# Attention values as seven block products in a decoder block kernel, with the second pair's gates and scores behind them

## The chip, the cores and the metric

The kernel runs on one core of one Trainium2 chip. The metric is the device time of one execution in microseconds. TensorE (PE) does the matmuls and transposes, VectorE (DVE) and ScalarE (ACT) the elementwise work, GpSimd (POOL) a few small steps, and SyncE (SP) issues nearly all transfers.

## What is computed

One decoder layer on x (512 x 1024, float32). One wide projection gives nine parts; two token mixers work on them, and their gated sum goes through two matmul stages with layer norms:

```
p = x @ W_in + b_in            # u | v | q | k | value | r | low rank | gate A | gate B
y_A = gelu(u) * (tril(W_s) @ layer_norm(gelu(v)) + b_s)      # in chunks of 128 positions, 8 groups
y_B = rms_norm(gla(q, k, value, log_sigmoid(...) / 16)) * gn * silu(r)    # 4 heads, chunked
m = sigmoid(gate_A) * y_A + sigmoid(gate_B) * y_B
h = layer_norm(alpha * x + m @ W_out)
out = layer_norm(alpha * h + relu(h @ W_1)^2 @ W_2)
```

## The kernel before

Every large matmul is done in three passes of reduced-precision operands: an operand is split into a high part, cast on ScalarE (`split`, line 88), and a low part, a subtraction on VectorE (line 89), and high x high, high x low and low x high are summed in a bank of PSUM. Weights come as a stream of 128 x 1024 pieces (`_stream`, `load_to`, `split_to`): SP loads a raw piece into one of three buffers, and the split fills one of seven pairs `wh`, `wl`. `split_to(n)` makes the pieces up to n, so each unit of matmuls asks for pieces up to seven ahead of its own. In the feed-forward, the second matrix is multiplied in seven block products instead of eight (Strassen-Winograd: `product_of`, `accumulators`, `operand`), with sums of weight pieces (line 128) in four held buffers A0, A1, B0, B1; each product is 24 matmuls.

The first part is a row of jobs, numbered by slots (`slot`), one for each bank of PSUM that is filled: the first q and k (a prologue), v (slots 0 to 7), u (8 to 15), the second pair's q and k (16 to 19), the attention values (20 to 27, two `row_unit`s of 96 matmuls, written to `bufB` by `copy_take`, line 786), gate A (`ga`, 28 to 35), then r and gate B (`r`, `gb`, 36 to 51, two and two: `branch`). A `col_job` is 24 matmuls on one weight piece. Side work is planned into slots by `at(n, f, phase)`: MM after the job's matmuls on TensorE, MAIN behind it, and LATE behind the next weight split. Instructions of TensorE, VectorE, ScalarE and GpSimd stand in the order in which this Python issues them; nothing is reordered there. SP's transfers are placed by a scheduler.

The side work of a pair of heads (`plan_pair`): gates (`gates_a`, `gates_b`), the parts between chunks (`inter_*`, `kd_turn`), three levels of scores (`level_diff`, `level_kdiff`, `level_exp`, `level_prep`, `level_score`: a difference of cumulated gates, its exponential, products with q and k, then eight matmul records `sc`), and diagonal scores (`diag_*`: products `dr`, their cast and low part `dt`, then the matmuls `sd`). Scores are copied into `AT` under masks (lines 501 to 533), and `chunk_out` makes the outputs and states per chunk. The two pairs are `pr0` and `pr1`.

PSUM has eight banks: four main ones (`ps_m`) for the jobs, two for scores and turned values (`ps_s`, one tile at a time), two for other side work (`ps_a`, tag `aux`). `r_take` turns the values' outputs on TensorE (`yt`) into the scores' tile.

## Time and profile before

| | |
|---|---|
| median of 3 runs | 756.06 us (755.71 to 756.31) |
| profiled execution | 755.66 us, span 753.9 us |
| TensorE busy | 745.6 us (99%), 3498 records of matmuls |
| VectorE busy | 473.7 us (63%) |
| ScalarE busy | 343.7 us (46%) |
| DMA | 85.14 MB, 113 GB/s on average |

Busy time is a share of the whole span; stages differ. A matmul of 512 columns is shown with some 0.39 us, but the next starts after 0.227 us, so times on TensorE are read from starts, as the chain does. An operand on a row such as `wl<-raw,wh` is what is written, then what is read.

### The profile page before, as it was taken

To read this page: it belongs to the slowest core of one execution; us is meant where nothing else is said; L and a number is where in the kernel's file an instruction comes from. 1 tells how busy PE (TensorE), PEld (TensorE's weight loads), DVE (VectorE), ACT (ScalarE), POOL (GpSimd) and SP (SyncE) were. 2 spreads that over 40 slices of the span, in tenths; PEclk is the share of its full clock that TensorE was granted. 3 is DMA by queue.
4 is the path that set the end of the run, shared out by engine and by line. 5 is a ranking of instruction groups with operands and counts; after the bars stand their busy time and mean duration, and the time that the engine had idled before them with its cause. 6 is when DMAs were issued, how large, how long until landed. Compare 5 with 4: busy or idle time off the path is not lost.

```text
span 753.9 us, 8782 instructions
## 1 busy us (share of the span) xinstructions
PE 745.6 (99%) x3498; PEld 626.2 (83%) x3498; DVE 473.7 (63%) x592; ACT 343.7 (46%) x450; POOL 29.9 (4%) x60
## 2 busy tenths in 40 slices
PE   9999999999999999999999999999999999999996
PEld 8888888888888888888888988888888888888885
DVE  7379867677575644445468523777567856687645
ACT  7476754363254745454222545454444454445300
POOL 1000000000000112000002000000000000000001
PEclk9999999999999999999999999999999999999998
DMA  8633421222141132522340314145331634145111
GB/s 342 214 124 126 153 82 61 82 84 84 49 146 58 56 126 85 183 96 85 98 159 33 115 62 151 41 140 196 113 111 39 240 107 145 56 121 202 41 57 56
DMA packets 25464, 85.14 MB, mean 113 GB/s; under 512 B 3088, under 2 KB 3344, under 8 KB 25424
## 3 DMA queue, kind: packets, MB, share of 16 engines
q1 hardware_dynamic: 25280, 84.33, 32.9%
q8 instruction: 27, 0.44, 0.2%
q10 hardware_dynamic: 144, 0.26, 0.1%
q14 instruction: 13, 0.11, 0.0%
HBM read 82.48 MB, written 2.10 MB: 112 GB/s over the span
## 4 chain that ended last, share of the span: by engine, by line
PE 97%; issue 1%; DVE 1%; POOL 0%; DVEq 0%; POOLq 0%
PE f L692 22%; PE ps L218 17%; PE mx L975 9%; PE f L1075 6%; PE gb L692 6%; PE r L692 6%; PE ga L692 6%; PE u L692 6%; PE mv L975 4%; PE qk L692 3%; PE first L276 3%; PE m L975 2%; PE sc L520 2%; PE pm L745 1%; PE po L554 1%
## 5 line engine op out<-in xcount | busy, mean ns | idle before, releaser
L89 DVE TENSOR_TENSOR wl<-raw,wh 128x1024 fp32r<-128x1024 f32 x141 | 171.1, 1223 | 114.3 <-ACT wh L88 112.5
L88 ACT CAST wh<-raw 128x1024 fp32r<-128x1024 f32 x141 | 145.6, 1044 | 49.0 <-PE ps L218 23.7
L692 PE MATMUL f<-xh,wh 128*128 128x512 f32 (+1 forms) x288 | 105.4, 366 | 0.0
L692 PE MATMUL f<-xl,wh 128*128 128x512 f32 (+1 forms) x288 | 105.3, 365 | 0.0
L692 PE MATMUL f<-xh,wl 128*128 128x512 f32 (+1 forms) x288 | 105.2, 365 | 0.0
L692 PEld LDWEIGHTS f<-xl,wh 128*128 128x128 f32 x288 | 54.3, 189 | 8.8
L692 PEld LDWEIGHTS f<-xh,wh 128*128 128x128 f32 x288 | 54.3, 189 | 8.7
L692 PEld LDWEIGHTS f<-xh,wl 128*128 128x128 f32 x288 | 54.3, 189 | 8.7
L915 ACT ACTIVATE F<-f 128x512 f32<-128x512 f32 (+1 forms) x28 | 15.0, 537 | 79.9 <-PE f L692 79.1
L218 PE MATMUL ps<-wh,xh 128*128 128x512 f32 x128 | 50.4, 394 | 0.0
L218 PE MATMUL ps<-wh,xl 128*128 128x512 f32 x128 | 49.9, 389 | 0.0
L218 PE MATMUL ps<-wl,xh 128*128 128x512 f32 x128 | 49.8, 389 | 0.0
L975 PE MATMUL mx<-wh,oh 128*128 128x512 f32 x96 | 37.3, 389 | 0.0
L975 PE MATMUL mx<-wl,oh 128*128 128x512 f32 x96 | 37.3, 389 | 0.0
L975 PE MATMUL mx<-wh,ol 128*128 128x512 f32 x96 | 37.3, 389 | 0.0
L128 DVE TENSOR_TENSOR raw<-raw,raw 128x1024 f32<-128x1024 f32 x24 | 29.2, 1218 | 2.8 <-DMA raw<-in_w_all 2.8
L218 PEld LDWEIGHTS ps<-wh,xl 128*128 128x128 f32 x128 | 24.0, 188 | 5.0
L218 PEld LDWEIGHTS ps<-wl,xh 128*128 128x128 f32 x128 | 24.0, 188 | 4.9
L218 PEld LDWEIGHTS ps<-wh,xh 128*128 128x128 f32 x128 | 24.0, 188 | 4.8
L692 PE MATMUL u<-xh,wh 128*128 128x512 f32 x64 | 25.9, 405 | 0.0
L692 PE MATMUL ga<-xh,wh 128*128 128x512 f32 x64 | 25.9, 404 | 0.0
L88 ACT CAST oh<-d 128x1024 fp32r<-128x1024 f32 x12 | 12.6, 1049 | 29.1 <-DVE d L948 29.1
(243 smaller groups left out, 1557.7 us busy)
## 6 DMA issues: line engine op xcount, KB each, us to landing
raw<-in_w_all SPq DMA_DIRECT2D x136, 512.0 KB, 3.3
bufB<-in_head SPq DMA_DIRECT2D x4, 512.0 KB, 7.6
xr<-in_x SPq DMA_DIRECT2D x8, 256.0 KB, 3.6
out<-bufA SPq DMA_DIRECT2D x8, 256.0 KB, 2.0
bufA<-in_head SPq DMA_DIRECT2D x3, 512.0 KB, 5.2
brow<-in_b_in SPq DMA_DIRECT2D x4, 256.0 KB, 6.4
g<-in_ln_g SPq DMA_DIRECT2D x2, 512.0 KB, 5.8
b<-in_ln_b SPq DMA_DIRECT2D x2, 512.0 KB, 5.5
```

The source lines that it names most:

```text
L88: nc.scalar.copy(hi, src)
L89: nc.vector.tensor_tensor(lo, src, hi.bitcast(F32), op=ALU.subtract)
L128: nc.vector.tensor_tensor(raw, x_, y_, op=ALU.subtract)
L218: nc.tensor.matmul(ps, s_, m_, start=(k == 0 and i == 0), stop=(k == KT - 1 and i == 2))
L276: nc.tensor.matmul(first[e], s_, m_[:, k, :], start=(k == 0 and i == 0), stop=(k == KT - 1 and i == 2))
L520: nc.tensor.matmul(sc[:, c, 0:192], pr.kt[:, jc * P : (jc + 1) * P], pr.qt[:, jc, :], start=True, stop=True)
L554: nc.tensor.matmul(po, pr.AT[:, j, c, :], vs, start=True, stop=(c == 0))
L692: nc.tensor.matmul(ps, s_, m_, start=(k == 0 and i == 0), stop=(k == KT - 1 and i == 2))
L745: nc.tensor.matmul(pm[:, c, :], bufB[:, c, gs], wst[:, g, :], start=True, stop=True)
L915: nc.scalar.activation(dst, ps, AF.Relu)
L975: nc.tensor.matmul(ps, s_, m_, start=(begins and k == 0 and i == 0), stop=(k == 3 and i == 2), skip_group_check=True,)
L1075: nc.tensor.matmul(ps, s_, m_, start=(f == 0 and i == 0), stop=(f == 7 and i == 2))
```

## The change

The attention values are computed in the same seven products as the feed-forward's second matrix. Their x operands are quarters of x, transposed, and sums of quarters; raw x is loaded into `bufB` (eight transfers, `operands_begin`) when the mixing has read it, summed there on VectorE (`x_sums`) and split (`x_parts`); weight sums use the held buffers, now open early. Products 1, 6, 7, 4 share main banks x, 5 and 3 main banks v, and product 2 uses the side work's banks (`aux`). Each result is added to a quarter of `bufB` (`value_take`, line 896 there). The look-ahead for weight pieces shrinks from 7 to 4 over the seven products and grows again in the first two `ga` jobs.

The main banks are now four named ones in turn (`bank`), and the turned values `yt` use one of them. The second pair's side work after `gates_a` moves from slots 18 to 35 to slots 25 to 42: behind the values, into `ga` and the first `r` and `gb`. The pair exponential for its diagonal scores is made ahead (`E1`). The order of the gates becomes r0 r1 gb0 gb1 r2 r3 gb2 gb3 gb4 to gb7, then r4 to r7, with the last four gates kept in `bufB`; products with the gate and sums (`onto`) follow.

```diff
-    ps_m = pool(ctx, "ps_m", bufs=4, space=PSUM)
+    ps_m = pool(ctx, "ps_m", bufs=1, space=PSUM)
...
+    turns = [0]
+
+    def bank(name, i=None):
+
+        if i is None:
+            i = turns[0]
+        turns[0] = (i + 1) % 4
+        return ps_m.tile([P, 512], F32, name=name, tag=f"ps{i}")
...
+    vgs = ExitStack()
+    held["pool"] = pool(vgs, "held_v", side="right")
...
+    quarter = lambda a, i, j: a[:, 2 * i : 2 * i + 2, 512 * j : 512 * j + 512]
+    GOES = {1: (0, 0), 2: (0, 0), 5: (1, 1), 6: (0, 1), 3: (0, 1), 7: (1, 1), 4: (1, 0)}
+    NEW = (1, 5, 6, 4)
+    made, sums = {}, {}
+
+    RAW_AT = {(1, 1): (0, 0), (0, 0): (1, 1), (0, 1): (0, 1), (1, 0): (1, 0)}
+
+    def xq(i, j):
+        return quarter(bufB, i, j).rearrange("p a (b n) -> p a b n", n=256)
...
+    def product_of(name, m, ops, take, of, ahead=W_BUFS):
+        hi, lo = ops
+        u0 = unit["next"]
+        unit["next"] = u0 + 2
+        split_to(u0 + 2)
+        banks, begins = accumulators(m, name, of)
...
+            for k in range(4):
...
+                if t and k % 2:
+                    split_to(u0 + k // 2 + 1 + ahead)
+            take(m, t, ps)
...
-        pass
+        E = None
...
+        for j in range(2 if pr.E is not None else 0):
+            nc.scalar.activation(pr.E[:, j, :], par(pr.lf, j, 1), AF.Exp, scale=1.0 / TEMP)
...
-        nc.scalar.activation(pr.raw[:, 512:768], par(pr.lf, j, 1), AF.Exp, scale=1.0 / TEMP)
+        if pr.E is None:
+            nc.scalar.activation(pr.raw[:, 512:768], par(pr.lf, j, 1), AF.Exp, scale=1.0 / TEMP)
...
-        nc.vector.tensor_mul(pair, pair, par(pr.q, j, 1))
+        first_ = pair if pr.E is None else pr.E[:, j, :]
+        nc.vector.tensor_mul(pair, first_, par(pr.q, j, 1))
...
+    def operands_begin():
+
+        sgu.close()
+        vgp = pool(vgs, "vgp", side="left")
+        vgp.tile([P, 120], F32, name="pad_v")
+        for (i, j), (a, b) in RAW_AT.items():
+            for k in range(2):
+                k0 = 4 * j + 2 * k
+                nc.sync.dma_start(xq(a, b)[:, k], head[:, k0 : k0 + 2, 256 * i : 256 * i + 256])
+        return vgp
+
     def second_parts():
-        sgu.close()
+        vgs.close()
+        held.clear()
         pr1.pool = gp1 = pool(gla, "gla_p1", side="left")
         pr1.AT = gp1.tile([P, 2, NCH, P], F32, name="AT1")
         nc.gpsimd.memset(pr1.AT, 0.0)
         pr1.QI = gp1.tile([P, 2, T], F32, name="QI1")
         pr1.KD = gp1.tile([P, 2, NCH, P], F32, name="KD1")
         pr1.et = gp1.tile([P, 2 * NCH], F32, name="et1")
+        pr1.E = gp1.tile([P, 2, T // 2], F32, name="E1")
...
-    S_VG, S_GA = 20, 28
-    S_R, S_O = 36, 52
+    S_VG, S_GA = 20, 27
+    S_R, S_O = 35, 51
...
-    def col_job(name, take):
+    def col_job(name, take, ahead=W_BUFS):
...
-        split_to(u0 + 1 + W_BUFS)
+        split_to(u0 + 1 + ahead)
...
-    at(S_U + 9, second_parts, phase=LATE)
+    at(S_U + 9, lambda: made.update(pool=operands_begin()), phase=LATE)
+    at(S_VG + 6, second_parts)
     at(S_U + 9, lambda: gates_a(pr1), phase=MM)
-    plan_pair(pr1, (18, 19, 20, 21), ((21, 23, 24, 25), (25, 27, 28, 29), (29, 30, 31, 32)), 32)
-    for n, pr, c in [(28, pr0, 0), (31, pr0, 1), (32, pr0, 2), (33, pr0, 3)] + [(36 + c, pr1, c) for c in range(NCH)]:
+    plan_pair(pr1, (25, 26, 27, 28), ((28, 30, 31, 32), (32, 34, 35, 36), (36, 37, 38, 39)), 39)
+    for n, pr, c in [(27, pr0, 0), (30, pr0, 1), (31, pr0, 2), (32, pr0, 3)] + [(43 + c, pr1, c) for c in range(NCH)]:
...
+    X_SUMS = (
+        ((0, 0), (1, 0), (0, 0), ALU.add),
+        ((1, 0), (1, 1), (1, 0), ALU.subtract),
+        ((1, 1), (0, 0), (1, 1), ALU.subtract),
+        ((0, 1), (0, 1), (1, 1), ALU.subtract),
+    )
+
+    def x_sums(n0, n1):
+        for o, a, b, op_ in X_SUMS[n0:n1]:
+            nc.vector.tensor_tensor(quarter(bufB, *o), quarter(bufB, *a), quarter(bufB, *b), op=op_)
+
+    def x_parts(m):
+        hi, lo = (
+            made["pool"].tile([P, 4, 256], F32R, name=f"x{c}{m}", tag=f"x{c}{m in (6, 7)}") for c in "hl"
+        )
+        split(*(a.rearrange("p (a b) n -> p a b n", a=2) for a in (hi, lo)), xq(*{5: (0, 0), 6: (1, 1), 3: (0, 1), 7: (1, 0)}[m]))
+        made[m] = hi, lo
+
+    at(S_VG - 1, lambda: x_sums(0, 1), lambda: x_parts(5))
+    at(S_VG - 1, lambda: x_sums(1, 3), phase=LATE)
...
-    def copy_take(half, br):
-        def f(t, ps):
-            nc.vector.tensor_add(bufB[:, t, half * 512 : (half + 1) * 512], ps, br)
-
-        return f
-
-    for half in range(2):
-        row_unit(xh, xl, copy_take(half, bias_row(C_VG + half * 512)))
+    brs = [bias_row(C_VG + half * 512) for half in range(2)]
+    b0 = turns[0]
+
+    def value_bank(name, kind, t):
+        if kind == "m":
+            return ps_a.tile([P, 512], F32, name=name, tag="aux")
+        return bank(name, (b0 + t + 2 * (kind == "v")) % 4)
+
+    def value_take(m, t, ps):
+        dst = quarter(bufB, *GOES[m])[:, t, :]
+        nc.vector.tensor_add(dst, brs[GOES[m][1]] if m in NEW else dst, ps)
+
+    for n, m in enumerate(ORDER):
+        if m == 5:
+            x_parts(6)
+            x_sums(3, 4)
+        elif m in (6, 3):
+            x_parts({6: 3, 3: 7}[m])
+        if m in (1, 2, 4):
+            i, j = {1: (0, 0), 2: (0, 1), 4: (1, 1)}[m]
+            ops = [a[:, 4 * j : 4 * j + 4, 256 * i : 256 * i + 256] for a in (xh, xl)]
+        else:
+            ops = made.pop(m)
+        product_of(f"v{m}", m, ops, value_take, value_bank, W_BUFS - n // 2)
+        pump(MM, MAIN)
+        pump(LATE)
+    turns[0] = (b0 + 2) % 4
     for e in range(KT):
-        col_job(f"ga{e}", ga_take(e))
+        col_job(f"ga{e}", ga_take(e), W_BUFS - max(0, 2 - e))
...
-            pt = ps_s.tile([P, 2, NCH, P], F32, name=f"yt{e}", tag="sc")[:, 0]
+            pt = bank(f"yt{e}").rearrange("p (c s) -> p c s", s=P)
...
-    def gb_take(e, t1):
+    def onto(e, gate, t1):
+        nc.vector.tensor_mul(t1, t1, gate)
+        nc.vector.tensor_add(AT_[:, e, :], AT_[:, e, :], t1)
+
+    def gb_take(e, gate, t1=None):
         def f(ps):
-            tm = temp(f"gb{e}")
-            nc.scalar.activation(tm, ps, AF.Sigmoid, bias=col("gb", e))
-            nc.vector.tensor_mul(tm, tm, t1)
-            nc.vector.tensor_add(AT_[:, e, :], AT_[:, e, :], tm)
+            nc.scalar.activation(gate, ps, AF.Sigmoid, bias=col("gb", e))
+            if t1 is not None:
+                onto(e, gate, t1)
...
-    def branch(e0):
+    for e0 in (0, 2):
         t1 = {e: temp(f"t1_{e}", "brow") for e in (e0, e0 + 1)}
         for e in t1:
             col_job(f"r{e}", r_take(e, t1[e]))
         for e in t1:
-            col_job(f"gb{e}", gb_take(e, t1[e]))
-            if e0:
-                split(mh[:, e, :], ml[:, e, :], AT_[:, e, :])
-
-    branch(0)
+            col_job(f"gb{e}", gb_take(e, temp(f"gb{e}"), t1[e]))
+
+    gate = {e: bufB[:, e - 4, 0:512] for e in range(4, KT)}
+    for e in gate:
+        col_job(f"gb{e}", gb_take(e, gate[e]))
     gla.close()
...
-    for e in range(2):
+    for e in range(4):
         split(mh[:, e, :], ml[:, e, :], AT_[:, e, :])
-    for e in range(2, KT, 2):
-        branch(e)
+    for e in gate:
+        t1 = temp(f"t1_{e}", "brow")
+        take = r_take(e, t1)
+
+        def parts_take(ps, e=e, t1=t1, take=take):
+            take(ps)
+            onto(e, gate[e], t1)
+            split(mh[:, e, :], ml[:, e, :], AT_[:, e, :])
+
+        col_job(f"r{e}", parts_take)
...
+    def ff_bank(name, kind, t):
+        return bank(name) if kind == "m" else ps_t.tile([P, 512], F32, name=name, tag=f"{kind}{t}")
...
-        b = lambda i, j: f2 + 8 * p + 2 * (2 * (i - 1) + j - 1) + h
+        if p < 0:
+            b = lambda i, j: 20 + 4 * (j - 1) + 2 * (i - 1) + h
+        else:
+            b = lambda i, j: f2 + 8 * p + 2 * (2 * (i - 1) + j - 1) + h
...
+    out += [operand(-1, m, h) for m in ORDER for h in range(2)] + plain(28, n)
...
-    part += [per_tile(w_in[:, c + c0 : c + c0 + 256]) for c0 in range(0, 1024, 256) for c in (C_R, C_GB)]
+    part += [per_tile(w_in[:, c + c0 : c + c0 + 256]) for c0 in (0, 256) for c in (C_R, C_GB)]
+    part += [per_tile(w_in[:, c + 512 : c + 1024]) for c in (C_GB, C_R)]
```

Three places in the order of the instructions. First VectorE at the start of the values. `qt`, `kd` and `QI` belong to the second pair's scores, `wl` are low weight parts, line 786 (896 after the change) takes a result into `bufB`. Before:

```order
L89 TENSOR_TENSOR wl30_1343<-raw30_1208,wh30_1342 128x1024
L786 TENSOR_TENSOR bufB_92<-ps_24_0_1353,brow_1351 128x512
L402 TENSOR_TENSOR QI1_1269<-QI1_1269,q1_1163 128x1024
L403 TENSOR_TENSOR kd1_1340<-kd1_1340,k1_1164 128x1024
L786 TENSOR_TENSOR bufB_92<-ps_24_1_1381,brow_1351 128x512
L425 TENSOR_TENSOR qt1_0_1417<-cum1_1298 128x8x96
L410 COPY KD1_1270<-pt1_0_1407 128x512
L410 COPY KD1_1270<-pt1_1_1412 128x512
L437 TENSOR_TENSOR kt1_0_1421<-cum1_1298 128x1024
```

After the change (`xl5`, `xl6`: low parts of x for products 5 and 6; line 865 sums quarters of x, line 128 weight pieces):

```order
L89 TENSOR_TENSOR xl5_1342<-bufB_92,xh5_1341 128x1024
L128 TENSOR_TENSOR raw25_866<-raw31_1165,raw25_866 128x1024
L89 TENSOR_TENSOR wl30_1346<-raw24_864,wh30_1345 128x1024
L865 TENSOR_TENSOR bufB_92<-bufB_92 128x2x512 x2
L896 TENSOR_TENSOR bufB_92<-brow_1354,mxv1_0_1358 128x512
L89 TENSOR_TENSOR wl31_1380<-raw25_866,wh31_1379 128x1024
L89 TENSOR_TENSOR wl32_1392<-raw30_1163,wh32_1391 128x1024
L896 TENSOR_TENSOR bufB_92<-brow_1354,mxv1_1_1359 128x512
L896 TENSOR_TENSOR bufB_92<-bufB_92,mv2_0_1396 128x512
L128 TENSOR_TENSOR raw30_1163<-raw30_1163,raw34_1312 128x1024
L89 TENSOR_TENSOR wl33_1418<-raw31_1165,wh33_1417 128x1024
L128 TENSOR_TENSOR raw31_1165<-raw31_1165,raw35_1350 128x1024
```

The second pair's products are gone from here, and sums and splits of x and weight sums stand between the takes; two more rows (a weight piece, the second take of product 2) follow before `xl6`.

Second, VectorE between the last level's difference of k (`kt`, line 437, 503 after the change) and its preparation. Before:

```order
L437 TENSOR_TENSOR kt1_2_1772<-cum1_1298 128x1024
L712 TENSOR_TENSOR bufA_91<-bufA_91,ga1_1754 128x512
L458 TENSOR_TENSOR qt1_2_1761<-qt1_2_1761,q1_1163 128x128x6
L460 TENSOR_TENSOR qt1_2_1761<-qt1_2_1761,whole1_2_1774 128x128x4
L460 TENSOR_TENSOR qt1_2_1761<-qt1_2_1761,whole1_2_1774 128x128x2
L465 TENSOR_TENSOR kt1_2_1772<-kt1_2_1772,k1_1164 128x1024
```

After the change:

```order
L503 TENSOR_TENSOR kt1_2_2181<-cum1_1593 128x1024
L935 TENSOR_TENSOR t1_0_2085<-t1_0_2085,gb0_2187 128x512
L936 TENSOR_TENSOR bufA_91<-bufA_91,t1_0_2085 128x512
L524 TENSOR_TENSOR qt1_2_2170<-qt1_2_2170,q1_1170 128x128x6
L526 TENSOR_TENSOR qt1_2_2170<-qt1_2_2170,whole1_2_2183 128x128x4
L526 TENSOR_TENSOR qt1_2_2170<-qt1_2_2170,whole1_2_2183 128x128x2
L531 TENSOR_TENSOR kt1_2_2181<-kt1_2_2181,k1_1171 128x1024
```

Two rows on gate B's first result (`gb0`) stand where one on `ga1` stood.

Third, the second pair's last diagonal score (`dr1_1`, `dt1_1`). ScalarE before:

```order
L711 ACT_TABLE_LOAD
L711 ACTIVATE ga6_2037<-ga6_2012,cols_sb_101 128x512
L482 CAST dt1_1_2044<-dr1_1_2006 128x768
L88 CAST wh45_2048<-raw45_1875 128x1024
L711 ACTIVATE ga7_2083<-ga7_2058,cols_sb_101 128x512
```

ScalarE after the change, and VectorE behind it:

```order
L940 ACT_TABLE_LOAD
L940 ACTIVATE gb2_2364<-gb2_2365,cols_sb_101 128x512
L550 CAST dt1_1_2398<-dr1_1_2362 128x768
L88 CAST wh59_2402<-raw59_2264 128x1024
L940 ACTIVATE gb3_2411<-gb3_2412,cols_sb_101 128x512
```

```order
L935 TENSOR_TENSOR t1_2_2269<-t1_2_2269,gb2_2364 128x512
L936 TENSOR_TENSOR bufA_91<-bufA_91,t1_2_2269 128x512
L548 TENSOR_TENSOR dr1_1_2362<-E1_1645,q1_1170 128x256
L549 TENSOR_TENSOR dr1_1_2362<-dr1_1_2362,k1_1171 128x256
L89 TENSOR_TENSOR wl59_2403<-raw59_2264,wh59_2402 128x1024
L569 COPY_PREDICATED AT1_1640<-masks_283,sd1_0_2393 128x512
L574 COPY_PREDICATED AT1_1640<-masks_283,sd1_0_2393 128x256
L553 TENSOR_TENSOR dt1_1_2398<-dr1_1_2362,dt1_1_2398 128x768
```

The products of `dr1_1` (lines 548 and 549) now stand behind the two rows on `gb2`.

## Rows read from the trace of the kernel before

**Rows 1.** The page, part 4: shares of the chain that ended last, by engine.
```profile
PE 97%; issue 1%; DVE 1%; POOL 0%; DVEq 0%; POOLq 0%
```

**Rows 2.** The chain in order of time (start us, us, what): values, one feed-forward product, last piece.
```profile
159.70 10.88 PE ps L218 x48
...
480.02 5.44 PE m L975 x24
...
703.06 43.84 PE f L1075 x216
```

**Rows 3.** Groups by line and shape: busy us, mean ns of one, idle before.
```profile
L89 DVE TENSOR_TENSOR wl<-raw,wh 128x1024 fp32r<-128x1024 f32 x141 | 171.1, 1223 | 114.3 <-ACT wh L88 112.5
...
L88 ACT CAST wh<-raw 128x1024 fp32r<-128x1024 f32 x141 | 145.6, 1044 | 49.0 <-PE ps L218 23.7 <-DMA raw<-in_w_all 11.3 <-PE mx L975 9.9
...
L786 DVE TENSOR_TENSOR bufB<-ps,brow 128x512 f32<-128x512 f32 x8 | 5.5, 689 | 11.7 <-PE ps L218 11.7
...
L481 DVE TENSOR_TENSOR dr<-dr,k 128x256 f32<-128x256 f32 x4 | 1.7, 426 | 0.1
```

**Rows 4.** Timeline of DVE in the feed-forward (start us, us, engine, line, operation).
```profile
474.35 1.23 DVE L89 TENSOR_TENSOR wl<-raw,wh 128x1024 fp32r<-128x1024 f32 x1
475.49 1.22 DVE L128 TENSOR_TENSOR raw<-raw,raw 128x1024 f32<-128x1024 f32 x1
...
477.76 0.68 DVE L992 SCALAR_TENSOR_TENSOR bufB<-bufA,mx 128x512 f32<-128x512 f32 x1
478.36 1.22 DVE L128 TENSOR_TENSOR raw<-raw,raw 128x1024 f32<-128x1024 f32 x1
```

**Rows 5.** Timelines of DVE, then ACT, around the start of the values.
```profile
156.79 1.23 DVE L89 TENSOR_TENSOR wl<-raw,wh 128x1024 fp32r<-128x1024 f32 x1 [3.55 <-ACT wh L88]
157.94 1.22 DVE L378 TENSOR_TENSOR lf<-lf,ab 128x1024 f32<-128x1024 f32 x1
159.19 2.63 DVE L382 TENSOR_TENSOR_SCAN cum<-ones,lf 128x128 f32<-128x128 f32 x8
...
155.73 1.03 ACT L88 CAST wh<-raw 128x1024 fp32r<-128x1024 f32 x1
...
159.73 0.69 ACT L347 ACTIVATE k<-qk,cols_sb 128x512 f32<-128x512 f32 x1 [1.45 <-PE qk L692]
```

**Rows 6.** Chain, ACT and DVE timelines: second pair's last level of scores.
```profile
220.66 1.30 PE sc L520 x8
...
232.85 1.30 PE sc L520 x8
...
226.12 1.06 ACT L451 ACTIVATE kt<-kt 128x1024 f32<-128x1024 f32 x1 [1.15 <-DVE kt L437]
...
226.54 0.95 DVE L458 TENSOR_TENSOR qt<-qt,q 128x768 f32<-128x768 f32 x1
...
228.60 1.22 DVE L465 TENSOR_TENSOR kt<-kt,k 128x1024 f32<-128x1024 f32 x1
```

**Rows 7.** Chain, ACT and DVE timelines: second pair's diagonal scores.
```profile
258.84 0.70 PE sd L494 x4
...
265.06 0.48 DVE dt L485
...
260.30 0.82 ACT L482 CAST dt<-dr 128x768 fp32r<-128x768 f32 x1
...
264.54 0.98 DVE L485 TENSOR_TENSOR dt<-dr,dt 128x768 fp32r<-128x768 f32 x1
```

**Rows 8.** Timeline of ACT: a table load ahead of a silu, and the silu.
```profile
326.04 1.28 ACT L801 ACT_TABLE_LOAD   x1 [2.69 <-PE r L692]
327.33 0.69 ACT L801 ACTIVATE t<-r,cols_sb 128x512 f32<-128x512 f32 x1
```

**Rows 9.** Stretches at the end: busy us per engine, granted clock (PEclk), DMA share, GB/s.
```profile
748.00:749.00 1.00, 0.00 (x0) 0.00 (x0) 0.96 (x4) 0.00 (x0) 0.65 (x1) 0.94 0.00 0
749.00:750.00 1.00, 0.00 (x0) 0.00 (x0) 1.00 (x2) 0.00 (x0) 0.34 (x1) 0.50 0.00 0
```

More of the change, by code (lines that the diff above doesn't have):

```diff
@@ L238, in hybrid_block @@
     sg = pool(sgu, "sgu", side="left")
-    first = [ps_m.tile([P, 512], F32, name=f"first{e}", tag="ps") for e in range(4)]
+    vgs = ExitStack()
+    held["pool"] = pool(vgs, "held_v", side="right")
+    first = [bank(f"first{e}") for e in range(4)]
     u0 = unit["next"]
@@ L319, in bias_row, with accumulators @@
         return row_bcast(rowp, b_in[c : c + 512], 512, "brow")
+    quarter = lambda a, i, j: a[:, 2 * i : 2 * i + 2, 512 * j : 512 * j + 512]
[5 more added lines that the diff above has]
+        return quarter(bufB, i, j).rearrange("p a (b n) -> p a b n", n=256)
+    def accumulators(m, name, of):
+        if m in (1, 6, 7, 4):
+            if m == 1:
+                sums["x"] = [of(f"mx{name}_{t}", "x", t) for t in range(2)]
+            return sums["x"], m == 1
+        if m in (5, 3):
+            if m == 5:
+                sums["v"] = [of(f"mv{name}_{t}", "v", t) for t in range(2)]
+            return sums["v"], m == 5
+        return [of(f"m{name}_{t}", "m", t) for t in range(2)], True
+    def product_of(name, m, ops, take, of, ahead=W_BUFS):
[4 more added lines that the diff above has]
+        banks, begins = accumulators(m, name, of)
+        for t, ps in enumerate(banks):
+            tsl = slice(t * P, (t + 1) * P)
+            for k in range(4):
+                wh, wl = (c.rearrange("p (k n) -> p k n", k=2)[:, k % 2, :] for c in chunks[u0 + k // 2])
+                for i, (s_, m_) in enumerate(passes(hi[:, k, tsl], lo[:, k, tsl], wh, wl)):
+                    nc.tensor.matmul(
+                        ps,
+                        s_,
+                        m_,
+                        start=(begins and k == 0 and i == 0),
+                        stop=(k == 3 and i == 2),
+                        skip_group_check=True,
+                    )
+                if t and k % 2:
+                    split_to(u0 + k // 2 + 1 + ahead)
+            take(m, t, ps)
     a_sb = sg.tile([P, T], F32R, name="a_sb")
@@ L933, in take_raw @@
         return lambda e, tsl, ps: square_to(F[:, j, e, tsl], ps)
-    GOES = {1: (0, 0), 2: (0, 0), 5: (1, 1), 6: (0, 1), 3: (0, 1), 7: (1, 1), 4: (1, 0)}
-    NEW = (1, 5, 6, 4)
-    made, sums = {}, {}
     def operand(F, p, m):
@@ L1114, in _stream @@
     n = 15 * 4
-    out = [(None, None, None, None, None)] * 4 + [(c, None, None, None, None) for c in range(n)]
+    plain = lambda a, b: [(c, None, None, None, None) for c in range(a, b)]
+    out = [(None, None, None, None, None)] * 4 + plain(0, 20)
     f1 = n
```

41 lines of the change are left out of this document (6 added, 35 removed).

## Prediction

> **What bounds the kernel now.** I read the chain of waits first. TensorE holds 97% of it [rows 1], and in order of time its matmul pieces follow each other with hardly a gap: 24 matmuls of 512 columns take 5.44 us (0.227 us each), in the value units as in the feed-forward products [rows 2]. So a matmul that is taken away is worth its whole 0.227 us, and every new wait of TensorE is lost in full. The question is then whether VectorE (DVE) and ScalarE (ACT) still deliver in time. For that I read, in this order, what their operations cost [rows 3], at what distance VectorE really starts them when its queue is full [rows 4], when it is free at the start of the values [rows 5], and the two places where TensorE waits on a short chain through both engines [rows 6, 7].
>
> Two things are to be seen in the queue. A 1024-wide operation lasts 1.22 us, but the next one starts 1.14 us after it; a 512-wide one lasts 0.68 and the next starts after 0.60 [rows 4]. If an operation needs what the one before it wrote, the distance is the full length: the 1.22 us operation at 157.94 is followed at 159.19, 1.25 us later [rows 5].
>
> **What is saved.** The values go from 192 matmuls (two units of 96) to 7 x 24 = 168. Saved: 24 x 0.227 = 5.44 us. No other matmul is added or lost; scores, transposes and outputs only change places.
>
> **The values' queue on VectorE.** Before, a value unit gives VectorE four weight pieces and four takes. Now there are 14 pieces instead of 8, 14 takes instead of 8, eight weight differences, four sums of x and four splits of x. The gates' 3.9 us (one difference, eight scans [rows 5]) leave this stage for a place where little else runs. The weight pieces are made up to seven ahead, which hides much, but the splits of x are made one product ahead, in the middle of the queue. Let me follow it, with TensorE starting the values at 159.70 as before [rows 2], since nothing ahead of them changes on its path.
>
> The piece whose cast runs at 155.73 behind the gates' logarithm starts on VectorE at 156.79, as before [rows 5]. Behind it come a weight difference that overwrites what this piece read (start 158.04), the next piece (159.18), the first sum of x (160.32 to 161.54), then its cast on ScalarE, 1.05, and the split xl5 can start at 162.65. From there to the end of xl6 stand, by the order: eight 1024-wide steps of 1.14, three of 1.25 (the next one depends on them), four takes of 0.60, and xl6 itself with 1.22: 16.5 us, end at 179.1. TensorE wants xl6 at the third matmul of the fourth product: 159.70 + 3 x 5.44 + 0.45 = 176.5. It waits 2.7 us. From the start of xl6 (177.9) to the end of xl7 come six steps of 1.14, two of 1.25, four takes and 1.22, 13.0 us: end at 190.9. TensorE without waits wants xl7 at 159.70 + 5 x 5.44 + 0.45 = 187.35. So the values end **3.5 us** late in all; the last 0.8 falls before the fifth and sixth products. No take is waited for: where products 7 and 4 share a bank without another between them, the take of the first half of product 7 ends two microseconds before product 4 writes there. Bounds: all steps at 1.14 and 0.60 gives 2.7, all at full length (some 14 steps by 0.11 and eight by 0.09 more) 5.7. I take 3.5, which uses each distance where a row shows it.
>
> What else changes here costs nothing. The main banks x and v and the two side banks of product 2 were read before 160 (the last mixing is taken at 152.6). The eight loads of x (256 KB) stand in SP's queue ahead of weights: the four for columns 0 to 511 go out when mixing group 3 is done, long before; the other four wait for the last mixing at 148.3 and hold up only pieces that the queue reaches after 170. Four more weight loads than before go out over 38 us.
>
> **The last level of scores.** Before, the score at 232.85 follows a preparation that starts at 226.54 and whose last product ends at 229.82; so 3.0 us to spare [rows 6]. Measured from the end of a column group (220.66), the exponential ends after 6.5 us and the preparation starts after 5.9. In the new place that group is r1: its own silu and product with the turned values stand in front of the difference, some 0.5 more, so the exponential ends at 7.05. And between difference and preparation now stand the sigmoid of gb0 with its table load (1.28 + 0.69 [rows 8]) and, on VectorE, a product and a sum (0.72 + 0.60, lengths as in [rows 3]). The preparation starts at 10.4 instead of 5.9, 4.5 later; the transposes give TensorE 0.4 more work before. 4.5 - 3.0 - 0.4 = **1.1 us** of waiting. Bounds 0 and 2.2 (a queue that is a further operation late).
>
> **The diagonal scores.** Before, the second one waits 0.56 us for its low parts [rows 7]: the chain is cast at 260.30, 1.46 after the matmuls ended at 258.84, then weight cast, weight piece, two masked copies, the difference, ended at 265.52, 5.2 after the cast began. Now the group ahead is gb2. Its table load waits for its matmuls, as two of the silu loads do: 2.69 idle before the load itself, the activation right behind [rows 8]. So: load 1.28, sigmoid 0.69, product and sum 1.42, two half-width products 0.9 [rows 3], and the cast starts 4.3 after the matmuls' end instead of 1.46. From the cast on the order is the same. All of it is 2.8 us later, and since TensorE already waits here, the wait grows by **2.8 us**. The exponentials made ahead (E1) take two table loads and two activations off ScalarE, but they were not the last to come. Bounds: 1.5 (the load doesn't wait), 3.4.
>
> **The clock.** These gaps, 2.7 and some 3.3 us, are longer than any in the trace but the end. There, TensorE's last piece ends at 746.9 [rows 2], the granted clock is 0.94 from 748 to 749 and 0.50 after [rows 9]: it fell from 2.4 to 1.2 GHz two microseconds after the last matmul. So it may fall in either gap, and the matmuls behind run at half rate for a time that no row shows. If it rises as slowly as it fell, a fall costs 1 us, less in the values, where TensorE would wait for xl7 anyway; a whole product at half rate would cost 5.4. Near the low end, I take 1.2 in all; bounds 0 and 5.4.
>
> **The sum.** Against the profiled execution, 755.66 us: -5.44 + 3.5 + 1.1 + 2.8 + 1.2 = +3.2, **758.8 us**. The median of the runs is 756.06, 0.4 above this execution, and a measurement of this kernel can tell about 0.2% (1.5 us) from no change: slower from 757.6, faster below 754.5. Low ends together give 755.66 - 5.44 + 2.7 + 0 + 1.5 = 754.4, but ends don't meet; this case alone lies between 756.5 and 761.5.
>
> Steps of 1.14 carry the values' term, and one rule speaks against them. In the Trainium skill, "VectorE: DVE Perf Modes", section Terms, a drain follows every VectorE operation, and the next can't issue until the pipe is empty. By that each step would be a full length, the values 5.7 late and the time 761.0. The trace differs: starts 1.14 apart for a length of 1.23 [rows 4].
>
> **Rivals.**
> - *The clock stays up.* Same waits without the 1.2: 757.6. For it: one row alone shows a fall, and TensorE works on both sides of the gaps. Chance 0.24.
> - *The scores come in time* (faster). If ScalarE's load before gb2 and the group before the last level don't hold the chain, because the precomputed exponential frees more of ScalarE than I count, neither score waits longer than before: 755.66 - 5.44 + 3.5 = 753.7, less the old 0.56: 753.2. It decides once the cast of dt starts within 1.5 us of gb2's end. Against it: a product and a sum with gb2 stand ahead of the diagonal's products in VectorE's order. Chance 0.17.
> - *The values' queue is in time.* The splits of x come before TensorE wants them: 758.8 - 3.5 = 755.3, and 754.1 if the clock stays up as well. It needs VectorE 2.7 us earlier at xl6. Against: sixteen operations stand in order from 162.65 on. Chance 0.09.
> - *Full lengths.* VectorE starts nothing early in this mix: 761.0. Against: [rows 4]. Chance 0.05.
> That the change doesn't do what it says is no rival here: TensorE's order holds 168 matmuls for the values. The whole 5.44 us (750.2) would need all three chains to be wrong.
>
> **Numbers.** Forecast 0.45. Slower by over 0.2% (above 757.57): nine tenths of it, half of the clock's rival, all of full lengths: 0.41 + 0.12 + 0.05, so 0.57. Faster by over 0.2% (under 754.55): most of the scores' rival and half of the queue's, 0.15 + 0.05, and 0.03 for the unseen: 0.23. Within: 0.20. The range, 753.0 to 761.4, takes in the forecast's own, full lengths and the rivals' points; outside lie the faster cases' lower halves and a clock that stays low for longer.
>
> **What would show it.** In the changed profile TensorE's pieces of the values should still be 5.44 for 24, with an idle piece of 2 to 3 us ended by xl6 early in the fourth product and small ones at xl3 and xl7; VectorE without idle time from 163 to 191; a wait of about 1 us before sc of the last level and about 3 us at the second sd, ended by dt; the granted clock under 1.00 near one of the gaps. The forecast is wrong if VectorE shows idle time inside 163 to 179, if xl6 ends before 177, if the table load before gb2 starts before its matmuls end, or if the largest new gap is in front of ga or po, where I cost nothing: the pieces of ga are made three or more groups ahead, and po needs only values that were taken.

## The result, and where the 5 us went

The change takes 761.2 us (median of 4 runs, 760.64 to 761.55) against 755.94 for the kernel before (median of 4 runs): 1.0068 times as long, 95% interval 1.0051 to 1.0086. The forecast was 758.8 with a range of 753.0 to 761.4, slower by over 0.2%. The profiled execution of the change took 760.64 us with a span of 758.9, 5.0 more than before.

The page of the change, parts 1 and 4 (busy time; shares of the chain):

```profile
PE 743.8 (98%) x3474; PEld 623.0 (82%) x3474; DVE 502.6 (66%) x620; ACT 348.1 (46%) x456; POOL 29.8 (4%) x60
...
PE 88%; DVE 5%; ACT 2%; issue 2%; DMA 1%; POOL 0%; DVEq 0%; ACTq 0%; POOLq 0%
```

The 24 matmuls are gone (3474 records instead of 3498), but TensorE's share of the chain fell from 97% [rows 1] to 88%: 5% now lies with VectorE, 2% with ScalarE. TensorE's waits, by what ended them (us in total, times, the longest):

```profile
PE mxv L373 <- DVE xl L89: 2.4, 1, 2.4
PE sd L562 <- DVE AT L574: 2.4, 1, 2.4
PE sc L588 <- DVE kt L531: 1.3, 1, 1.3
...
PE sd L562 <- DVE dt L553: 0.2, 1, 0.2
```

Left out are 1.1 us at the very start, which the kernel before has too, and 0.2 us for the high part `xh6` on ScalarE. Beside the start, the kernel before had one such wait, 0.2 us for `dt`. All three forecast places are there: the fourth value product (`mxv`, waiting for `xl6`), the last level's score (`sc`) and the second diagonal score (`sd`).

**The values.** TensorE's timeline, with the first value matmul, the one that waited and the first of gate A (start us, us, line, operation):

```profile
160.12 0.39 PE L373 MATMUL mxv<-wh,xh 128*128 128x512 f32 x1
...
179.93 0.59 PE L373 MATMUL mxv<-wh,xl 128*128 128x512 f32 x1 [2.44 <-DVE xl L89]
...
202.95 0.39 PE L773 MATMUL ga<-xh,wh 128*128 128x512 f32 x1
```

Seven products of 5.44 are 38.08 us; from 160.12 to 202.95 it took 42.83, so 4.75 were lost. The third matmul of product 6 was wanted at 160.12 + 16.32 + 0.45 = 176.9 and started at 179.93, 3.0 late. VectorE's timeline says why:

```profile
178.66 1.22 DVE L89 TENSOR_TENSOR xl<-bufB,xh 128x1024 fp32r<-128x1024 f32 x1
179.79 1.22 DVE L865 TENSOR_TENSOR bufB<-bufB 128x1024 f32<-128x1024 f32 x1
...
184.59 1.22 DVE L89 TENSOR_TENSOR xl<-bufB,xh 128x1024 fp32r<-128x1024 f32 x1
...
190.67 1.22 DVE L89 TENSOR_TENSOR xl<-bufB,xh 128x1024 fp32r<-128x1024 f32 x1
```

`xl6` is the row at 178.66, `xl3` at 184.59, `xl7` at 190.67. From 163.3 to 194.2 VectorE had no idle time. The granted clock (PEclk, third number from the right) in the stretches around the wait:

```profile
179.00:180.00 1.00, 0.07 (x1) 0.07 (x1) 1.00 (x2) 0.00 (x0) 0.00 (x0) 1.00 0.65 254
180.00:181.00 1.00, 1.00 (x3) 0.82 (x4) 1.00 (x1) 0.00 (x0) 0.00 (x0) 0.60 0.00 0
181.00:182.00 1.00, 1.00 (x3) 0.74 (x3) 0.90 (x3) 0.84 (x1) 0.00 (x0) 0.50 0.00 0
...
184.00:185.00 1.00, 1.00 (x6) 0.84 (x5) 1.00 (x3) 0.07 (x1) 0.00 (x0) 1.00 0.73 209
```

It fell to 0.50, that is from 2.4 to 1.2 GHz, just when work came again after the wait (1.00 from 179 to 180, 0.60 in the next microsecond), and was back at 1.00 by 184. Behind 179.93 the matmuls start 0.43 us apart instead of 0.227.

**The last level's score.** The chain in order of time (start us, us, what):

```profile
277.66 1.06 ACT kt L517
278.74 1.28 ACT L940
280.03 0.70 ACT gb L940
280.75 0.70 DVE t L935
281.48 0.69 DVE bufA L936
282.17 0.88 DVE qt L524
...
285.51 1.54 PE sc L588 x8
```

Behind the exponential (277.66) come the table load and the sigmoid of `gb0`, then the two `onto` rows on `t` and `bufA`, and only at 282.17 the preparation. In [rows 6] it started 0.4 us into the exponential.

**The second diagonal score**, the same view:

```profile
305.75 1.28 ACT L940
307.04 0.70 ACT gb L940
307.76 0.70 DVE t L935
308.49 0.69 DVE bufA L936
...
310.01 0.83 ACT dt L550
...
313.73 0.72 DVE AT L574
314.45 0.79 DVE dt L553
```

The load starts when the matmuls of `gb2` end, as forecast. The cast of the products `dr` starts at 310.01, 4.28 us after them, where 4.3 was forecast and 1.46 stood in [rows 7]. TensorE's wait is ended first by the masked copy at 313.73, which frees the one tile for scores, and 0.7 later by `dt`.

All of it together, by the starts of TensorE's matmuls in the two profiles:

| place | before | after | difference |
|---|---|---|---|
| first matmul of the values | 159.53 | 160.12 | +0.59 |
| from there to the first of the output projection | 206.28 | 209.88 | +3.60 |
| from there to the last matmul | 380.80 | 381.42 | +0.62 |
| from there to the end of the span | 7.29 | 7.48 | +0.19 |

The 3.60 are -5.44 saved, +4.75 in the values, +1.26 at `sc`, +2.36 at the second `sd` (2.58 of waiting instead of 0.22, by the view of waits; the prediction's 0.56 for the latter was read from the chain), +0.40 at the first `sd` (its four rows took 1.10 instead of 0.71), and 0.27 in small pieces.

### The profile page after: what moved, and what is told of

Its sections match the earlier page's. It is cut to its first block, busy times and chain, and to the rows that moved or that the text cites. A ratio compares the mean times of both kernels' runs of the same rounds, so it can differ in the third digit from the quotient of the medians.

```text
span 758.9 us, 8814 instructions
## 1 busy us (share of the span) xinstructions
PE 743.8 (98%) x3474; PEld 623.0 (82%) x3474; DVE 502.6 (66%) x620; ACT 348.1 (46%) x456; POOL 29.8 (4%) x60
## 4 chain that ended last, share of the span: by engine, by line
PE 88%; DVE 5%; ACT 2%; issue 2%; DMA 1%; POOL 0%; DVEq 0%; ACTq 0%; POOLq 0%
PE f L773 22%; PE ps L227 11%; PE mx L373 8%; PE r L773 6%; PE ga L773 6%; PE u L773 6%; PE f L1165 5%; PE mv L373 4%; PE gb L773 4%; PE first L287 3%; PE mxv L373 2%; PE m L373 2%; PE sc L588 2%; DVE wl L89 2%; PE qk L773 1%
## 5 line engine op out<-in xcount | busy, mean ns | idle before, releaser
L89 DVE TENSOR_TENSOR wl<-raw,wh 128x1024 fp32r<-128x1024 f32 x147 | 178.1, 1222 | 122.8 <-ACT wh L88 121.6
L88 ACT CAST wh<-raw 128x1024 fp32r<-128x1024 f32 x147 | 151.5, 1044 | 54.8 <-PE ps L227 15.6
L128 DVE TENSOR_TENSOR raw<-raw,raw 128x1024 f32<-128x1024 f32 x32 | 39.0, 1219 | 2.9 <-DMA raw<-in_w_all 2.8
L773 PE MATMUL r<-xh,wh 128*128 128x512 f32 x64 | 25.8, 404 | 0.0
L773 PE MATMUL gb<-xh,wh 128*128 128x512 f32 x64 | 25.7, 402 | 0.0
L227 PE MATMUL ps<-wh,mh 128*128 128x512 f32 x64 | 25.2, 393 | 0.0
L227 PE MATMUL ps<-wh,xh 128*128 128x512 f32 x64 | 25.2, 393 | 0.0
L773 PE MATMUL r<-xh,wl 128*128 128x512 f32 x64 | 25.0, 391 | 0.0
L773 PE MATMUL gb<-xh,wl 128*128 128x512 f32 x64 | 25.0, 391 | 0.0
```

Source lines behind the costliest of these rows:

```text
L88: nc.scalar.copy(hi, src)
L89: nc.vector.tensor_tensor(lo, src, hi.bitcast(F32), op=ALU.subtract)
L128: nc.vector.tensor_tensor(raw, x_, y_, op=ALU.subtract)
L227: nc.tensor.matmul(ps, s_, m_, start=(k == 0 and i == 0), stop=(k == KT - 1 and i == 2))
L773: nc.tensor.matmul(ps, s_, m_, start=(k == 0 and i == 0), stop=(k == KT - 1 and i == 2))
```

## The experiments

Each kernel is the changed kernel with the edit shown. Times are medians, with the ratio to the kernel before, timed on the same chip.

### e1_onto: the products with gate B behind the scores' steps

```diff
             if t1 is not None:
-                onto(e, gate, t1)
+                at(slot[0], lambda: onto(e, gate, t1))
```

> The changed kernel, with the product and the sum on gb0 to gb3 (the two VectorE rows of `onto`) issued behind the side work of the same slot instead of ahead of it; nothing is left out. Theory (the two score waits come from these rows standing in VectorE's queue ahead of the scores' chains): the preparation of the last level no longer stands behind 1.4 us of `onto` and the sigmoid it waits for, so the 1.26 us wait at its score goes; at the second diagonal score the half-width products run during gb2's sigmoid, the cast starts right behind it (about 2.0 us after gb2's matmuls end instead of 4.3) and the 2.36 us wait falls to 0.1 to 0.4, with 0.2 to 0.7 left at its second matmul as before. Time 761.2 - 1.26 - 2.2 = 757.7. Rival (ScalarE's table loads and sigmoids hold the chains, not VectorE's queue): the diagonal's wait stays above 1.5 us and the time is 759.5 or more.

Measured: 756.29 us over 11 runs, where 757.7 was expected; ratio 1.0004 (0.9995 to 1.0013): no different from the kernel before. The wait at `sc` is gone from the view. At the second `sd` the chain is now

```profile
303.33 1.28 ACT L940
304.63 0.69 ACT gb L940
305.32 0.72 ACT dt L550
...
310.50 0.74 PE sd L562 x3
```

The cast follows the sigmoid directly, 2.0 us after the matmuls' end, and what is left of the wait is 0.6 us in two parts, about as before the change. ScalarE's load and sigmoid still stand there, so the rival falls. At each of the two scores, two small VectorE rows, 1.4 us of work that nobody needed soon, had stood in the chain, waiting there for the gate's sigmoid; the two waits had been worth 1.26 + 2.36 = 3.6 us of TensorE's time. Between the two profiles (760.64 and 755.36 us) 3.88 us came back from gate A to the output projection, 0.48 ahead of the values, 0.49 from the output projection on, and 0.44 in the values. There the gap at `xl6` was as long as in the change, 2.84 us from start to start, but in the same stretch as above the clock stayed up:

```profile
176.61 0.40 PE L373 MATMUL mxv<-wl,xh 128*128 128x512 f32 x1
179.45 0.50 PE L373 MATMUL mxv<-wh,xl 128*128 128x512 f32 x1 [2.45 <-DVE xl L89]
...
180.00:181.00 1.00, 1.00 (x6) 0.82 (x5) 0.90 (x2) 0.31 (x1) 0.00 (x0) 1.00 0.00 0
```

The values then took 42.39 us: 4.31 lost without any fall of the clock, because `xl3` and `xl7` were waited for instead (0.2 and 0.4 us by the view). The fall had cost 0.44 net in the change's profile, as the time lost to slow matmuls there would have been spent waiting for VectorE.

### e2_x6: one split of x earlier

```diff
-        if m == 5:
+        if m == 2:
             x_parts(6)
+        elif m == 5:
             x_sums(3, 4)
```

> The changed kernel, with the split of x for the fourth product (xl6) one product earlier; nothing else moves and nothing is left out. Theory (VectorE's whole queue is too long between 160 and 192 us, as it has no idle time there): xl6 ends near 174 and is in time, but xl3 ends at 185.8 as before, where TensorE wants it at 182.3; the wait moves there, about 3.5 us, and some 0.6 more at xl7. The values gain at most 0.6 us of waiting, plus or minus the clock's 1.6 us according to whether it falls again in that gap: time 759.0 to 761.5. Rival (xl6's place alone is at fault): both the 2.8 us wait and the slow matmuls behind it go, 4.4 us, and the time is 756.8.

TensorE's waits for the values, from the view by what ended them:

```profile
PE mvv L373 <- DVE xl L89: 2.9, 1, 2.9
...
PE mxv L373 <- DVE xl L89: 0.3, 1, 0.3
PE mvv L373 <- ACT xh L88: 0.2, 1, 0.2
```

Measured: 762.51 us (760.38 to 763.64), ratio 1.008 (1.0067 to 1.0093). The wait went from `mxv` (product 6) to `mvv` (product 3): TensorE stood from 182.92 to 186.18 for `xl3`. The values took 42.39 us, as in e1_onto, so the rival, `xl6`'s place alone, is out. The queue as a whole is too long. The median is 1 us over the expected range; its five runs are spread over 3.3 us, and only the fastest was profiled, with the clock up in the values. That execution had a mean granted clock of 0.997, the other four 0.991 to 0.993, and they took 1.8 to 3.3 us longer. So TensorE had the lower clock for longer in them; at which gaps it fell isn't known.

### e3_lead: fewer weight pieces ahead as well

```diff
-        product_of(f"v{m}", m, ops, value_take, value_bank, W_BUFS - n // 2)
+        product_of(f"v{m}", m, ops, value_take, value_bank, W_BUFS - (0, 2, 2, 3, 3, 4, 4)[n])
...
-    col_job(f"ga{e}", ga_take(e), W_BUFS - max(0, 2 - e))
+    col_job(f"ga{e}", ga_take(e), W_BUFS - max(0, 3 - e))
```

(with the edit of e2_x6)

> As the run with the earlier split of x, and the weight pieces are made fewer ahead: 7, 5, 5, 4, 4, 3, 3 pieces in the seven products instead of 7, 7, 6, 6, 5, 5, 4, growing again over three gate jobs. Same work on every engine, nothing left out; only VectorE's order differs, with splits of x ahead of pieces that are wanted later. Theory (queue order and lead): xl6 ends at 174, xl3 near 183.3 against 182.3 wanted, xl7 near 188 against 188.8; one wait of about 1.0 us is left of the values' 3.1, and a gap that short leaves the clock up, so the values end 3.7 us earlier: 757.5. Rival (total work of VectorE bounds the stage, whatever its order): weight pieces come late in their turn, the wait is at wl36 to wl39 or in the first gate jobs, and the time stays at 760 or above.

The same view of this kernel has one row on the values:

```profile
PE mvv L373 <- DVE xl L89: 1.1, 1, 1.1
```

Measured: 757.82 us over 11 runs, ratio 1.0018 (1.0010 to 1.0027). One wait of 1.1 us at `xl3` is left in the values, which took 39.47 us: 1.39 lost instead of 4.75 (4.31 with the clock up). VectorE's work is the same, so it was the order: weight pieces wanted two products later stood ahead of splits wanted now.

### e4_fill: TensorE busy through the wait

```diff
+        if m == 6:
+            keep = ps_s.tile([P, 512], F32, name="keep", tag="sc")
+            for _ in range(12):
+                nc.tensor.matmul(keep, ops[0][:, 0, 0:P], xh[:, 0, :], start=True, stop=True)
         product_of(f"v{m}", m, ops, value_take, value_bank, W_BUFS - n // 2)
```

> The changed kernel, with twelve extra matmuls (128x512, results unused, in the bank of the scores, which is free there) ahead of the fourth product: TensorE then works through the time in which it waited for xl6. Everything that is waited for stays. Theory (the eight matmuls behind the gap take 0.43 us instead of 0.227 because the clock fell to 1.2 GHz in the gap): the granted clock stays 1.00, the matmuls behind xl6 are 0.227 apart, the wait for xl6 is still over at 179.9, and the values end 1.6 us earlier; but then xl3 and xl7 are wanted 1.6 us earlier too, ends 185.8 and 191.9 against 185.4 and 190.9, so up to 1.0 is lost again: 759.6 to 760.6. Rival (the slowness is the operands' arrival or the restart itself): 761.2, matmuls still 0.43 apart behind xl6.

Measured: 761.4 us (760.82 to 761.5), ratio 1.0065 (1.0053 to 1.0078): no gain. In the values the clock stayed at 1.00 and they took 42.44 us, 0.39 less than in the change's profile, where at least 0.6 was expected: the time went into later waits. But this execution's clock fell at the other gap, ahead of the second diagonal score (stretches as above):

```profile
314.00:315.00 1.00, 0.23 (x1) 0.26 (x1) 1.00 (x2) 0.13 (x1) 0.00 (x0) 0.75 0.63 164
315.00:316.00 1.00, 1.00 (x2) 0.53 (x3) 1.00 (x2) 0.00 (x0) 0.00 (x0) 0.50 0.89 360
316.00:317.00 1.00, 1.00 (x5) 0.84 (x4) 0.97 (x3) 0.00 (x0) 0.00 (x0) 0.50 0.00 0
...
318.00:319.00 1.00, 1.00 (x6) 0.79 (x6) 0.96 (x2) 0.00 (x0) 0.00 (x0) 1.00 0.17 41
```

There nothing was waited for afterwards, and the fall cost in full: the score and the next column group took 1.72 + 6.13 us, in the change's profile 1.26 + 5.47, so 1.1 us. The rival, that a restart as such is slow, falls with e1_onto, where the same restart with the clock up had matmuls 0.227 us apart from the second on. Keeping TensorE busy through one wait gained little here, because it was about to wait again; whether it pays where no wait follows wasn't tried.

### e5_both and e6_idle: the edits together, and one sum of x in idle time

e5_both is e1_onto and e3_lead together. e6_idle adds:

```diff
-    at(S_VG - 1, lambda: x_sums(0, 1), lambda: x_parts(5))
-    at(S_VG - 1, lambda: x_sums(1, 3), phase=LATE)
+    at(S_U + 9, lambda: x_sums(0, 1), phase=MM)
+    at(S_VG - 2, lambda: x_parts(5))
+    at(S_VG - 2, lambda: x_sums(1, 3), phase=LATE)
...
+    at(S_U + 6, lambda: operands_load(0), phase=LATE)
```

(`operands_load(0)` issues the four loads of columns 0 to 511, taken out of `operands_begin`.)

> The two edits that each gave time back, together: `onto` behind the slot's side work, and the earlier split of x with fewer weight pieces ahead. Nothing is left out. Theory (the waits are separate, one queue in the values, one in the scores, and TensorE's order is the same): the gains add up, 756.29 - (761.2 - 757.82) = 752.9; in the profile about 1.1 us of waiting at xl3 is left in the values and 0.5 us at the second diagonal score, as before the change. Rival (VectorE's work put off in the values comes due in the gate jobs and hits the scores): a new wait at qt, kt or a weight piece between 200 and 310 us, 754.5 or more.

> As e5_both, and the first sum of x moves into VectorE's idle time ahead of the values (its four loads are issued three jobs earlier, the split for the third product and the next two sums one job earlier). Nothing is left out. Theory (the last 1.1 us of waiting in the values is VectorE's queue after 160 us, and that queue gets 1.1 us shorter and loses a 1.2 us pause for the cast): the wait at xl3 goes, 751.8, and a wait of at most 0.2 us at a split of x is left. Rival (what is left at xl3 is set by its place behind the takes, which wait for TensorE): 752.9 as e5_both.

Measured: e5_both 752.85 us (752.77 to 753.34), ratio 0.9957 (0.9944 to 0.9969); e6_idle 751.45 us (751.01 to 752.48), ratio 0.9936 (0.9922 to 0.9949). Both are faster than the kernel before, by 0.4% and 0.6%. For e5_both the view of TensorE's waits still has this on the values:

```profile
PE mvv L373 <- DVE xl L89: 1.1, 1, 1.1
```

For e6_idle it has only this behind the start:

```profile
PE f L1171 <- DVE wl L89: 0.4, 1, 0.4
PE sd L562 <- DVE dt L553: 0.2, 1, 0.2
```

The gains added up to 0.1 us of what was expected for e5_both. In e6_idle no wait is left in the values: from their first matmul to the first of gate A they took 38.08 us, seven products and nothing else.

```profile
160.37 0.39 PE L373 MATMUL mxv<-wh,xh 128*128 128x512 f32 x1
...
198.45 0.39 PE L776 MATMUL ga<-xh,wh 128*128 128x512 f32 x1
```

So VectorE can do all of this work beside TensorE; neither rival holds.

### e7_noE: each diagonal score makes its own exponential again

```diff
-        pr1.E = gp1.tile([P, 2, T // 2], F32, name="E1")
```

(on e1_onto)

> As the run with `onto` behind the side work, without the pair exponential made ahead: each diagonal score makes its own again, so that two loads of the exponential's table and two activations come back between the gates' activations, and two loads of theirs follow. Nothing is left out. By the prediction (those were not the last to come): 756.3, waits as in e1_onto. Rival (they would stand ahead of the casts): the second exponential waits for the buffer that the first score's low part reads, then sigmoid's table is loaded again behind it, and the cast starts some 0.8 us later; at the first score the silu waits for a reload, up to 1.3 us; 757.1 to 758.4, with those waits at sd.

ScalarE at the second diagonal score:

```profile
303.64 1.28 ACT L542 ACT_TABLE_LOAD   x1 [2.20 <-DVE dt L553]
...
305.39 1.28 ACT L939 ACT_TABLE_LOAD   x1
...
307.27 0.82 ACT L550 CAST dt<-dr 128x768 fp32r<-128x768 f32 x1
```

Measured: 759.11 us (757.37 to 759.87), ratio 1.0032 (1.0020 to 1.0045), 2.8 more than e1_onto in the medians and 2.0 in the profiles (757.37 against 755.36). The median is 0.7 above the rival's range: the two executions with a mean granted clock of 0.997 took 757.37 and 757.75, the three at 0.992 to 0.994 took 759.11 to 759.87. The exponential's load waits for `dt` of the first score, which still reads the buffer that the exponential is to fill, the sigmoid's table is loaded again behind it, and the cast starts at 307.27 instead of 305.21. All of the 2.0 us is the wait at the second `sd`; the first one did not change. So the rival holds: in this order the loads are the last to come, and `E1` is worth 2.0 us. The prediction's sentence that they were not the last was on the change's own order, with `onto` in front, and there it wasn't tried.

### e8_again: the change once more

> The changed kernel once more, without any edit, to see what of its first profile comes again. Expected of both views: waits of about 2.4 us at xl6, 1.26 at the last level's score and 2.4 at the second diagonal score come again to 0.1 us, as they follow from the order of the queues. If the clock's fall behind xl6 belongs to the gap's length, it comes again at the same place; if it is a matter of chance (the run with `onto` moved had the same gap of 2.84 us with the clock at 1.00 behind it), it may be missing or be found behind the other gap, and the time moves by some 0.5 to 1 us with it. The start of the values, 0.6 us later than before the change in the first profile although nothing ahead of it changed, comes again if it is the change's, and else not.

Measured: 761.92 us (760.26 to 763.0), ratio 1.0073 (1.0060 to 1.0085). The waits came again at 2.44, 1.26 and 2.36 us. So did the clock's fall behind `xl6`, as the stretch around it shows:

```profile
180.00:190.00 10.00, 9.58 (x35) 7.73 (x36) 9.73 (x11) 3.75 (x4) 0.00 (x0) 0.83 0.24 74
```

Yet e1_onto and e7_noE had this gap too (2.84 and 2.85 us), with the clock at 1.00 behind it. In the four profiles the gap began at 177.09 and 177.58 where the clock fell, and at 176.61 and 176.60 where it didn't. The length of a gap alone doesn't decide it; what does is open. The values started at 160.61 here, and between 159.64 and 160.69 in the other runs. All of the 0.59 us arises in the first 27 us, and from there to the values every profile takes 132.7 to 132.8 us. Runs whose instructions are the same up to the values differ by as much as that, so the 0.59 us can't be put down to the change; the kernel before has just one profile to compare.

### e9_casts: the two activations behind the casts

On e6_idle, the activation on `gb2` and the silu of `r3` with its product are deferred in the same way as `onto`. The edit on `gb2`:

```diff
-            nc.scalar.activation(gate, ps, AF.Sigmoid, bias=col("gb", e))
+            def use():
+                nc.scalar.activation(gate, ps, AF.Sigmoid, bias=col("gb", e))
+
+            if e == 2:
+                at(slot[0], use)
+            else:
+                use()
```

> As e6_idle, and the activations on r3 and on gb2 (with r3's product with the turned values) go behind the casts of the diagonal scores' products, so that these casts no longer wait for the end of a column group. Nothing is left out. Theory (what is left of waiting at the two diagonal scores, 0.4 us more than before the change at the first and about 0.6 at the second, stands behind these activations and gb2's table load): the first score's low part ends 2 us earlier and its wait goes; the second's cast starts right after its products, and its low part ends 0.8 us earlier, as the weight split and the copies in front of it stay; both waits go, 751.45 - 1.0 = 750.4. Rival (the second is held by the weight split behind gb2's activation, which stays in its place): only the first goes, 751.0.

The waits at the second score in the same view:

```profile
PE sd L562 <- DVE AT L574: 0.3, 1, 0.3
PE sd L562 <- DVE dt L553: 0.2, 1, 0.2
```

Measured: 751.69 us (751.05 to 751.92), ratio 0.9939 (0.9925 to 0.9952): no difference from e6_idle that these runs can tell. The first score lost its wait (its rows took 0.71 us, as before the change, instead of 1.11), and the second got a longer one, 0.3 for the masked copy beside 0.2 for `dt`: TensorE came 0.4 us earlier to a copy that stands where it stood, behind the weight split that waits for `gb2`'s activation. The rival had the mechanism; of its 0.4 us nearly all went into that wait.

## Why the prediction was right, and by how much it was off

The direction was right, the time fell into the range, and the mechanisms were the forecast ones; the sum was +3.2 us and the profile gave +5.0. At the forecast places the account came out close, +3.16 forecast and +3.60 measured, but there is luck in this: the values' queue was put 0.8 too low and the clock 0.8 too high. Another 1.4 us came from places that were given nothing, and the median ended 0.2 us short of the range's upper end.

- **What is saved**: 5.44 us, right. e6_idle, free of waits there, has values of exactly 38.08 us.
- **The values' queue**: 3.5 forecast, 4.31 with the clock up (e1_onto). `xl6` was to end at 179.1 against 176.5 wanted, and ended at 179.9 against 176.9, a wait of 3.0 for 2.7. Both engines came 0.59 us later than before: VectorE's first piece at 157.38 for 156.79, TensorE's first value matmul at 160.12 for 159.53. But the forecast had taken TensorE's start from the chain, 159.70, and so had given VectorE 0.17 too much time. From the start of `xl5` to that of `xl6` the queue took 15.34 for 15.25. The rest, 1.3 for 0.8, fell at products 3 and 7, as said: from the start of `xl6` to the end of `xl7` it took 13.23 for 13.0, and behind each wait the second matmul came 0.34 us after the first instead of 0.227, which was not counted. The lower bound of 2.7 for this term doesn't come out of its own steps: with 1.14 and 0.60 throughout they give 2.9. e2_x6 shows that it is the queue and not one row; e3_lead and e6_idle show that its order is to blame.
- **The last level's score**: 1.1 forecast, 1.26 measured. The preparation started 10.5 us behind the group's end, where 10.4 was forecast. e1_onto shows that it is `onto` with the sigmoid it waits for.
- **The diagonal scores**: 2.8 forecast at the second, 2.36 measured there and 0.40 at the first, which had been given nothing. The two belong together, as the second chain starts when `gb2`'s matmuls end, ahead of both scores: what TensorE loses at the first, it waits less at the second. e9_casts shows the same, with the 0.4 us going back to the second. The prediction had the wait ended by `dt`; the masked copy, which frees the tile, stands just ahead of `dt` in the same queue and ended most of it. The steps to the cast came out at 4.28 for 4.3. Of these, e1_onto left the load and the sigmoid in front of the cast, and took away only the product and the sum, behind which the half-width products stood; the wait fell to about what it was before the change. That the exponentials made ahead would not matter is wrong for e1_onto's order (e7_noE) and untested for the change's.
- **The clock**: 1.2 forecast, in one of the two gaps. In the profile it fell at the first, to the level that [rows 9] had shown, and cost 0.44 net, for the reason given in the prediction; at the second gap, in e4_fill, a fall cost 1.1. The profile is of the fastest of four executions; the others were not profiled, and the last section says what their times and clocks show.
- **Not forecast**: 0.59 us before the values, 0.62 from the output projection to the last matmul and 0.19 at the end, 1.4 of the 1.8 us by which the sum was short. The first varies between runs of the same instructions. Of the second, 0.45 is lost in the last stage, around one late weight piece. e2_x6, e3_lead, e6_idle and e8_again lost 0.3 to 0.7 there, the other runs 0.1 or nothing; the cause is open.

The rival "full lengths" gave 761.0, the nearest number to the result, but for a reason that the trace refutes: behind `xl6` at 178.66, 1.22 us long, the next operation starts at 179.79, 1.13 later, and so it is in this stage wherever the next operation doesn't touch what the one before it read or wrote. The rule of the Trainium skill, "VectorE: DVE Perf Modes", section Terms, that the next operation can't issue before the drain is over, doesn't show in these rows. The rivals in which a queue comes in time were wrong for this kernel, and became true by reordering. The scores' rival took off the old 0.56, although its own condition, no longer wait than before, gives 753.7. With both queues in time that leaves 753.7 - 3.5 = 750.2 us, and the best version, e6_idle, stands at 751.45.

## What to carry to other kernels

Where one engine is busy all the time, the work that a change adds elsewhere is not to be judged by that engine's busy share but by due times: list what stands in the helper's queue ahead of each operand that is waited for, and move what is due later behind it. Work that nobody awaits, such as a product into an accumulator, goes behind the steps of a chain that alternates between two engines; here two such rows at each of two scores cost 3.6 us of TensorE's time. And when a wait goes, look at the next row of the same queue before counting the gain: moving one split alone only moved the wait (e2_x6).

## What was not expected of the hardware

Around gaps of TensorE of 2.7 to 3.3 us, from start to start, the granted clock fell in some executions and not in others: behind `xl6` in two of four profiles with a gap of 2.84 us, around the second diagonal score in one of five profiles with 2.7 us (e4_fill; not the two of the change, nor e2_x6 and e3_lead), and not behind 3.26 us in e2_x6. Where it fell, it fell within a microsecond of the end of the gap: by stretches of half a microsecond some 0.3 us before the first matmul in e4_fill, 0.3 behind it in the change, and 0.9 behind it in e8_again, when TensorE was working again. Then it stood at 0.50 for some 3 us. This cost 1.1 us where nothing else was late, and 0.44 and 0.50 in the values, where VectorE was late anyway.

The executions that were not profiled were often slower, with a lower mean granted clock. The eight profiles without a fall ahead of the last matmul have means of 0.997, the three with one 0.994 and 0.995. The three other executions of the change had 0.993 to 0.995 and took 0.3 to 0.9 us more than the profiled one. e3_lead took 757.08 to 757.62 us in the five executions at 0.997 or above and 757.82 to 758.48 in the six at 0.994 and 0.995. e1_onto, whose only long gap between its start and its end is at `xl6`, took 755.36 to 756.29 in four executions at 0.997 or above and 756.90 to 757.11 in three at 0.993. The versions without such gaps, e5_both, e6_idle and e9_casts, stayed at 0.996 or above in all 15, and the kernel before at 0.997 to 0.999 in those timed beside them. So one profile may understate what the clock costs; where it fell in the other executions, and for how long, isn't known.
